# One hybrid layer on one core: the spill of the residual, the order of expert selection, and the layout of the sub keys changed

## The chip, the core and the metric

The program runs on 1 core of one Trainium2 chip. TensorE (PE) does the matrix products, VectorE (DVE) and ScalarE (ACT) the element-wise work, GpSimd (POOL) issues the gathers, and SyncE (SP) issues almost all other transfers, which 16 DMA engines carry out. The metric is the device time of one execution in microseconds (us), lower is better.

## What is computed

One layer on 512 tokens of 2048 features, float32. The first half (a retention branch and a dilated attention branch) yields `merged`. The change lies in the second half:

```python
x = x + merged @ w_out                       # residual
h2 = rms_norm(x, ffn_norm_g)
x = x + peer_ffn(h2, w_query, sub_keys, u, v)

def peer_ffn(h, w_query, sub_keys, u, v):    # 8 heads, 128 keys, 16384 experts
    q = (h @ w_query).reshape(B, S, 8, 256)
    s1 = einsum('bshd,hkd->bshk', q[..., :128], sub_keys[:, 0])
    s2 = einsum('bshd,hkd->bshk', q[..., 128:], sub_keys[:, 1])
    v1, i1 = top_k(s1, 16);  v2, i2 = top_k(s2, 16)
    best, pos = top_k(all sums v1 + v2, 16)
    experts = i1[pos // 16] * 128 + i2[pos % 16]
    gates = softmax(best)
    act = gelu(h . u[experts]) * gates       # 128 experts per token
    return sum of act * v[experts]
```

## The kernel before

The 512 tokens are four tiles of 128. The whole layer runs twice over its stages: part 0 for tile 0, part 1 for tiles 1 to 3. Tiles 0 and 1 then fetch the rows of their experts one by one with gathers (POOL, line 756; DVE multiplies each gathered row, lines 765 and 774, 2.3 us each). A gather step is let out by `tick` each time a part of a weight has been split (0.85 of a step) or a step of the gate tables is done (one step). Tiles 2 and 3 take another way: all 128 groups of 128 experts are multiplied out densely, which is the long last phase.

Matrix products use split numbers. `load_w` loads 256 rows of a weight (`wraw`, 512 KB, line 127, SP), ACT rounds it (`whi`, line 130) and DVE subtracts (`wlo`, line 131); three products per pair then go to PE (`gemm`, lines 146 to 148). One such weight part stands for 18 products of 128x512 with three tiles, and a chunk of 512 columns has eight parts. In the second half of the program there are four buffers for `wraw` and three for `whi` and `wlo`.

`merge` multiplies by `w_out` in four chunks (loop at 604). For each chunk and tile it loads the old residual (`xr`, line 609, three buffers), adds it to the product (line 610, DVE, written to `x1`), sends the sum to memory (`x1D`, line 611, SP), and squares it on ACT (line 612, into `xr`, with the sum of squares as a by-product). After the last chunk `x1` is scaled in place (line 623 on DVE for tiles 0 and 2, line 621 on ACT for tile 1), transposed (line 597), split (lines 567 and 568), and the first tile is multiplied by the norm's gains (`fgr`, lines 628 to 630, whose buffers are those of `xr`).

`routing` takes four chunks of queries. Each chunk c is a product with `w_query`, a copy (`qn`, 641), transposes (648, 650), scores against `skT` (653, 656), and then the selection on DVE: the top 16 of every half (lines 520 to 524), of their sums, a look-up of the expert numbers (695 to 703), and the softmax, whose exponential is on ACT (707). `routing_tables` (714 to 726) loads the sub keys in four pieces, transposes them on PE and copies them on ACT. Before the selection of chunk 3 the call `before_last` writes out the first NFIRST = 11 groups of dense experts (`expert_in`: `ur` from SP at 836, `uh` on ACT at 839, `ul` on DVE at 840, 48 products at 854 to 856). When the last selection is done, expert numbers and gates go through memory (`hk_T`, 888 to 900), and the stage of the gate tables `GD` follows, in four blocks of eight steps (912 to 928) with more dense experts between them. One further group closes the stage, so that 24 groups are done when the dense phase begins.

A scheduler orders each engine's instructions when the program is built; each engine then works through its own list strictly in that order, and waits where the next instruction waits. So the place of an instruction in a list decides what is held up behind it.

Of the kernel before, what the change touches and what calls it, by code (L numbers as in the profile page):

```python
# [10 lines left out]
F32 = mybir.dt.float32  # L11
BF16 = mybir.dt.bfloat16
F32R = mybir.dt.float32r
U32 = mybir.dt.uint32
I32 = mybir.dt.int32
AF = mybir.ActivationFunctionType
# [3 lines left out]
P = 128  # L20
# [6 lines left out]
H = 8  # L27
# [37 lines left out]
def hybrid_layer(ctx, tc, I, out, dbg=None):  # L65
    nc = tc.nc
# [33 lines left out]
    ident = const.tile([P, P], F32, name="ident")  # L100
# [3 lines left out]
    def bank(name, pool=None):  # L104
        return (pool or psB).tile([P, 512], F32, name=name, tag="bank")
# [49 lines left out]
    with tc.tile_pool(name="x0", bufs=1) as x0:  # L155
# [22 lines left out]
        for k in range(KT):  # L178
            ps = bank("xT")
# [25 lines left out]
    x1D = dram.tile([NT, P, D], F32, name="x1D")  # L205
# [334 lines left out]
    def merge(part, mg, pieces):  # L540


        t0, T = (0, 1) if part == 0 else (1, NT - 1)
# [34 lines left out]
        for c in range(4):  # L578
            cs = slice(c * 512, (c + 1) * 512)
            ps = gemm((I["w_ret_out"][0], c * 512, tiles(rT)))[0]  # L580
# [4 lines left out]
            ps = gemm((I["w_attn_out"][0], c * 512, tiles(aT)), nk=8)[0]  # L585
# [16 lines left out]
        ss4 = mg.tile([P, T, 4], F32, name="ss4")  # L602
        x1 = [mg.tile([P, D], F32, name=f"x1_{t}", tag=f"row{t}") for t in range(T)]
        for c in range(4):
            cs = slice(c * 512, (c + 1) * 512)
            ps = gemm((I["w_out"][0], c * 512, tiles(mT)))[0]
            for t in range(T):
                xr = mg.tile([P, 512], F32, name="xr", tag="xr", bufs=3)
                nc.sync.dma_start(xr, x4[t0 + t][:, cs])
                nc.vector.tensor_add(x1[t][:, cs], ps[t], xr)  # L610
                nc.sync.dma_start(x1D[t0 + t][:, cs], x1[t][:, cs])
                nc.scalar.activation(xr, x1[t][:, cs], AF.Square, accum_out=ss4[:, t, c:c + 1])
        fg = mg.tile([P, KT], F32, name="ffng")
        nc.sync.dma_start(fg, I["ffn_norm_g"][0].rearrange("(k p) -> p k", p=P))
        for t in range(T):
# [10 lines left out]
        for c in range(4):  # L626
            cs = slice(c * 512, (c + 1) * 512)
# [5 lines left out]
    def routing(T, rt, skT, tab, tiles2, before_last=None):  # L633

        N2 = 2 * T
        gates, e1, e2 = [rt.tile([P, T, 8, 16], F32, name=n, bufs=1) for n in ("gates", "e1", "e2")]
        for c in range(4):
            ps = paired((I["peer_w_query"][0], c * 512, tiles2))
            qn = rt.tile([P, T, 512], F32, name="qn", bufs=2)
            for t in range(T):  # L640
                nc.scalar.copy(qn[:, t], ps[t])
            v12 = rt.tile([P, T, 2, 2, 16], F32, name="v12")
            i12 = rt.tile([P, T, 2, 2, 16], U32, name="i12")
            scs = []
            for i in range(4):
                pt = bank("qT")
                for t in range(T):
                    nc.tensor.transpose(pt[:, t * P:(t + 1) * P], qn[:, t, i * P:(i + 1) * P], ident)
                qT = rt.tile([P, T * P], F32, name="qTs", bufs=2)
                nc.scalar.copy(qT, pt[:, :T * P])  # L650
                ss = bank("s12")
                for t in range(T):
                    nc.tensor.matmul(ss[:, t * P:(t + 1) * P], qT[:, t * P:(t + 1) * P], skT[:, 4 * c + i],
                                     start=True, stop=True)
                sc = rt.tile([P, T * P], F32, name="s12s", bufs=4)
                nc.scalar.copy(sc, ss[:, :T * P])
                scs.append(sc)
            if c == 3 and before_last:
                before_last()
            for i in range(4):  # L660
                for t in range(T):
                    scr = rt.tile([P, P], F32, name="scr")
# [14 lines left out]
            for a in range(N2):  # L677
# [32 lines left out]
            nc.vector.tensor_mul(gates.rearrange("p t (c u) k -> p t c u k", c=4)[:, :, c],  # L710
                                 ex.rearrange("p (t u) k -> p t u k", t=T),
                                 sm.rearrange("p (t u) -> p t u", t=T)[:, :, :, None].to_broadcast([P, T, 2, 16]))
        return e1, e2, gates

    def routing_tables(rt):
        tab = rt.tile([P, 3, 16], F32, name="tab", bufs=1)
        nc.sync.dma_start(tab.rearrange("p a b -> p (a b)"), bcast(I["c_rank"], 48))
        skT = rt.tile([P, 16, P], F32, name="skT", bufs=1)
        for q4 in range(4):
            sk = rt.tile([P, 4, P], F32, name="sk", bufs=1)  # L720
            nc.sync.dma_start(sk, I["peer_sub_keys"][0].rearrange("h s k d -> k (h s) d")[:, 4 * q4:4 * q4 + 4])
            ps = bank("skT")
            for i in range(4):
                nc.tensor.transpose(ps[:, i * P:(i + 1) * P], sk[:, i], ident)
            nc.scalar.copy(skT[:, 4 * q4:4 * q4 + 4].rearrange("p a b -> p (a b)"), ps)
        return skT, tab


# [63 lines left out]
    with tc.tile_pool(name="mgA", bufs=1, reuse_waits="tile") as mg, \  # L792
            tc.tile_pool(name="rtA", bufs=2, reuse_waits="tile") as rt, \
            tc.tile_pool(name="flA", bufs=2, reuse_waits="tile") as fl:
        skT, tab = routing_tables(rt)
# [24 lines left out]
    NV = 8  # L820
    NGRP = P // NV
    NPRE = 24
    NFIRST = 11
    NLAST = 1
    right = ctx.enter_context(ExitStack())
    pools = {}
# [38 lines left out]
    def begin_dense():  # L865
# [5 lines left out]
        load_u(0)  # L871
        for n in range(NFIRST):
            expert_in(n)

    with tc.tile_pool(name="mgO", bufs=1, reuse_waits="tile") as mgO:
# [5 lines left out]
        with tc.tile_pool(name="rtB", bufs=2, reuse_waits="tile") as rt:  # L881
            skT, tab = routing_tables(rt)
            e1, e2, gates = routing(3, rt, skT, tab, tiles2, begin_dense)
            unit(1, e1[:, 0], e2[:, 0], gates[:, 0], h2D)
            for i, src in enumerate((e1, e2, gates)):
                ps = bank("hkT")
# [8 lines left out]
    with tc.tile_pool(name="gb", bufs=1, reuse_waits="tile") as gb:  # L895
# [6 lines left out]
        for blk in range(NB):  # L902
# [3 lines left out]
            for o in range(TB // OB):  # L906
                t0 = blk * TB + o * OB
# [6 lines left out]
                for q in range(OB // 4):  # L914
                    ps = bank("gg")
# [101 lines left out]
def laid_out(inputs):  # L1017
    host = {n: np.ascontiguousarray(inputs[n]) for n in _INS}
    u = host["peer_u"].reshape(P, P, KT, P)
    host["u_feat"] = np.ascontiguousarray(u.transpose(0, 3, 2, 1)).reshape(P, P, KT * P)  # L1020
    host.update(shape_constants())
    return host

# [16 lines left out]
```

## Time and profile before

| | us |
|---|---|
| median of 3 runs (4589.60 to 4595.62) | 4591.96 |
| the profiled execution | 4602.08 |
| its span, first to last instruction | 4600.3 |
| stage: `w_out` of part 1 to the last sum | about 2600 to 2736 |
| stage: norm and transposes | 2736 to 2767 |
| stage: four query chunks and their scores | 2763 to 2968 |
| stage: dense experts up to the hand-over of the selection | 2968 to 3032 |
| stage: hand-over and gate tables | 3032 to 3271 |
| stage: dense phase | 3271 to 4600 |

Times in the trace count from the start of the span. In a timeline row the first number is the start, the second the duration; square brackets give how long the engine had stood idle before and what ended that. PEclk is the granted clock of TensorE as a share of 2.4 GHz, 0.5 being 1.2 GHz. A DMA share is the mean busy share of the 16 DMA engines.

### The profile page before, as it was taken

What the parts mean: (1) busy time and instruction counts of PE and PEld (TensorE: products, weight loads), DVE (VectorE), ACT (ScalarE), POOL (GpSimd) and SP (SyncE); (2) the same over time, 40 slices, a digit from 0 to 9 for tenths busy, and PEclk for the clock granted to TensorE, in tenths of its full rate; (3) what the DMA queues carried; (4) which work ended last, traced back from release to release, by engine and by line L of the source; (5) the groups of instructions that cost most, each with busy time, mean ns of one, the idle gap of its engine ahead of it and who ended that gap; (6) DMA issues with size and microseconds to landing.
All of it is one profiled execution on the core that took longest, in us unless ns stands there. A gap on an engine that the chain in (4) does not pass through costs nothing.

```text
span 4600.3 us, 57918 instructions
## 1 busy us (share of the span) xinstructions
PE 4211.8 (92%) x21638; PEld 3524.4 (77%) x21638; DVE 3439.3 (75%) x4495; ACT 1917.0 (42%) x2674; POOL 795.5 (17%) x516
## 2 busy tenths in 40 slices
PE   8999998988998999989979977886799999999999
PEld 6878776765776778767758866786689998899997
DVE  7454554546566878677678878888779998999997
ACT  6444555545442323443432333344434443344443
POOL 0000000000002112222122221012112332344332
PEclk9999999999999999999989998998899999999999
DMA  7666675758658889888899885267889999999997
GB/s 241 226 219 218 215 243 178 244 193 287 224 160 303 323 290 331 313 305 320 300 346 373 340 323 202 92 236 292 318 302 363 397 400 391 401 400 402 405 403 293
DMA packets 510171, 1358.78 MB, mean 295 GB/s; under 512 B 49216, under 2 KB 129088, under 8 KB 440768
## 3 DMA queue, kind: packets, MB, share of 16 engines
q1 hardware_dynamic: 432800, 816.00, 50.9%
q0 software_dynamic: 73728, 536.90, 29.7%
q8 instruction: 170, 2.79, 0.2%
q10 hardware_dynamic: 3360, 2.17, 0.2%
q14 instruction: 113, 0.93, 0.1%
HBM read 1290.05 MB, written 64.88 MB: 295 GB/s over the span
## 4 chain that ended last, share of the span: by engine, by line
PE 50%; DMA 18%; DVE 13%; issue 13%; ACT 3%; POOL 2%; SPq 0%; ACTq 0%; DVEq 0%; POOLq 0%
PE gB L147 9%; PE gB L148 9%; PE gB L146 9%; PE psy L981 3%; PE psy L982 3%; PE psy L980 3%; PE psa L856 3%; PE psa L854 3%; PE psa L855 3%; DMA gr<-in_peer_v,eid 3%; DMA ur<-in_u_feat 3%; DMA wraw<-in_w_in 2%; POOL gr L756 2%; DVE wlo L131 2%; DMA vr<-in_peer_v 2%
## 5 line engine op out<-in xcount | busy, mean ns | idle before, releaser
L131 DVE TENSOR_TENSOR wlo<-wraw,whi 128x1024 fp32r<-128x1024 f32 x752 | 917.2, 1223 | 650.6 <-ACT whi L130 636.0
L130 ACT CAST whi<-wraw 128x1024 fp32r<-128x1024 f32 x752 | 789.4, 1051 | 1227.7 <-PE gB L148 913.6
L756 POOL DMA_INDIRECT gr<-in_peer_u,eid x256 | 362.9, 1418 | 2752.8 <-DVE eid L743 1535.1
L774 DVE SCALAR_TENSOR_TENSOR accg<-gr,wg,accg 128x2048 f32<-128x2048 f32 x256 | 600.5, 2346 | 50.6 <-DMA gr<-in_peer_v,eid 38.5
L765 DVE SCALAR_TENSOR_TENSOR gr<-gr,hrow 128x2048 f32<-128x2048 f32 x256 | 583.8, 2284 | 45.7 <-DMA gr<-in_peer_u,eid 44.2
L854 PE MATMUL psa<-rh,uh 128*128 128x256 f32 x2048 | 582.1, 284 | 29.6 <-ACT uh L839 29.6
L756 POOL DMA_INDIRECT gr<-in_peer_v,eid x256 | 432.4, 1689 | 994.8 <-DVE accg L774 929.1
L856 PE MATMUL psa<-rh,ul 128*128 128x256 f32 x2048 | 581.8, 284 | 9.8 <-DVE ul L840 9.8
L855 PE MATMUL psa<-rl,uh 128*128 128x256 f32 x2048 | 580.0, 283 | 0.0
L839 ACT CAST uh<-ur 128x1024 fp32r<-128x1024 f32 x256 | 268.9, 1051 | 479.0 <-DMA ur<-in_u_feat 381.1
L981 PE MATMUL psy<-vl,wh 128*128 128x512 f32 x1024 | 405.1, 396 | 19.7 <-DVE vl L974 19.5
L854 PEld LDWEIGHTS psa<-rh,uh 128*128 128x128 f32 x2048 | 390.9, 191 | 34.7 <-ACT uh L839 30.5
L980 PE MATMUL psy<-vh,wh 128*128 128x512 f32 x1024 | 402.5, 393 | 6.0 <-ACT vh L973 5.9
L982 PE MATMUL psy<-vh,wl 128*128 128x512 f32 x1024 | 400.7, 391 | 0.0
L855 PEld LDWEIGHTS psa<-rl,uh 128*128 128x128 f32 x2048 | 397.6, 194 | 4.0
L856 PEld LDWEIGHTS psa<-rh,ul 128*128 128x128 f32 x2048 | 390.7, 191 | 12.2 <-DVE ul L840 12.0
L973 ACT CAST vh<-vr 128x1024 fp32r<-128x1024 f32 x256 | 267.9, 1050 | 300.6 <-DMA vr<-in_peer_v 164.5
L974 DVE TENSOR_TENSOR vl<-vr,vh 128x1024 fp32r<-128x1024 f32 x256 | 310.4, 1220 | 76.8 <-ACT vh L973 76.4
L147 PE MATMUL gB<-wlo,rh 128*128 128x512 f32 x768 | 316.3, 412 | 52.3 <-DVE wlo L131 52.0
L840 DVE TENSOR_TENSOR ul<-ur,uh 128x1024 fp32r<-128x1024 f32 x256 | 311.2, 1218 | 57.5 <-ACT uh L839 56.3
L146 PE MATMUL gB<-whi,rh 128*128 128x512 f32 x768 | 309.2, 406 | 31.5 <-ACT rh L570 22.7
L148 PE MATMUL gB<-whi,rl 128*128 128x512 f32 x768 | 311.0, 405 | 0.3 <-DVE rl L571 0.2
(467 smaller groups left out, 7957.5 us busy)
## 6 DMA issues: line engine op xcount, KB each, us to landing
wraw<-in_w_in SPq DMA_DIRECT2D x528, 512.0 KB, 5.0
ur<-in_u_feat SPq DMA_DIRECT2D x256, 512.0 KB, 9.6
vr<-in_peer_v SPq DMA_DIRECT2D x256, 512.0 KB, 9.9
wraw<-in_w_ret_out SPq DMA_DIRECT2D x64, 512.0 KB, 6.1
wraw<-in_w_out SPq DMA_DIRECT2D x64, 512.0 KB, 5.8
wraw<-in_peer_w_query SPq DMA_DIRECT2D x64, 512.0 KB, 4.9
wraw<-in_w_attn_out SPq DMA_DIRECT2D x32, 512.0 KB, 6.8
GD<-Gs SPq DMA_DIRECT2D x4, 4096.0 KB, 14.6
```

Source lines behind the costliest of these rows:

```text
L130: nc.scalar.copy(whi, raw)
L131: low = nc.vector.tensor_sub(wlo, raw, whi.bitcast(F32))
L146: nc.tensor.matmul(ps[t], ah(k), whi[:, j], start=first, stop=False)
L147: nc.tensor.matmul(ps[t], ah(k), wlo[:, j], start=False, stop=False)
L148: nc.tensor.matmul(ps[t], al(k), whi[:, j], start=False, stop=last)
L756: nc.gpsimd.indirect_dma_start(out=r, out_offset=None, in_=pu if s < P else pv_, in_offset=bass.IndirectOffsetOnAxis(ap=u.eid[:, s % P:s % ...
L765: nc.vector.scalar_tensor_tensor(r, r, 1.0, u.hrow, op0=ALU.mult, op1=ALU.mult, accum_out=u.ag[:, s:s + 1])
L774: nc.vector.scalar_tensor_tensor(u.acc, r, u.wg[:, s - P:s - P + 1], u.acc, op0=ALU.mult, op1=ALU.add)
L854: nc.tensor.matmul(psa[:, j], uh[:, cs], chi[k], start=k == 0, stop=False)
L855: nc.tensor.matmul(psa[:, j], uh[:, cs], clo[k], start=False, stop=False)
L856: nc.tensor.matmul(psa[:, j], ul[:, cs], chi[k], start=False, stop=k == KT - 1)
L981: nc.tensor.matmul(ps[:, t], wh[:, j, ts_], vl[:, j], start=False, stop=False)
```

## The change

Four edits.

1. The spill. The sum of line 610 is written into the loaded tile `xr`, and `x1D` is stored from there. ACT squares `xr` into `x1` and then copies `xr` to `x1`. `xr` is the buffer that the next loads of `xr` and `fgr` take.
2. The order of selection. `routing` is cut into `queries(c)` and `select(c)`, written in the order queries 0, queries 1, select 0, queries 2, select 1, queries 3, first dense experts, select 2, select 3. The scores `s12s` have eight buffers in place of four.
3. NFIRST is 16 in place of 11.
4. The host lays out the sub keys as `key_feat` (feature by key), and one transfer of 1 MB fills `skT`.

```diff
-                nc.vector.tensor_add(x1[t][:, cs], ps[t], xr)
-                nc.sync.dma_start(x1D[t0 + t][:, cs], x1[t][:, cs])
-                nc.scalar.activation(xr, x1[t][:, cs], AF.Square, accum_out=ss4[:, t, c:c + 1])
+                nc.vector.tensor_add(xr, ps[t], xr)
+                nc.sync.dma_start(x1D[t0 + t][:, cs], xr)
+                nc.scalar.activation(x1[t][:, cs], xr, AF.Square, accum_out=ss4[:, t, c:c + 1])
+                nc.scalar.copy(x1[t][:, cs], xr)
...
-        for c in range(4):
+        def queries(c):
+
             ps = paired((I["peer_w_query"][0], c * 512, tiles2))
...
-            v12 = rt.tile([P, T, 2, 2, 16], F32, name="v12")
-            i12 = rt.tile([P, T, 2, 2, 16], U32, name="i12")
             scs = []
...
-                sc = rt.tile([P, T * P], F32, name="s12s", bufs=4)
+                sc = rt.tile([P, T * P], F32, name="s12s", bufs=8)
                 nc.scalar.copy(sc, ss[:, :T * P])
                 scs.append(sc)
-            if c == 3 and before_last:
-                before_last()
+            return scs
+
+        def select(c, scs):
+            v12 = rt.tile([P, T, 2, 2, 16], F32, name="v12")
+            i12 = rt.tile([P, T, 2, 2, 16], U32, name="i12")
...
+        found = {}
+        for c in range(4):
+            found[c] = queries(c)
+            if c == 3 and before_last:
+                before_last()
+            if c > 0:
+                select(c - 1, found.pop(c - 1))
+        select(3, found.pop(3))
         return e1, e2, gates
...
-        for q4 in range(4):
-            sk = rt.tile([P, 4, P], F32, name="sk", bufs=1)
-            nc.sync.dma_start(sk, I["peer_sub_keys"][0].rearrange("h s k d -> k (h s) d")[:, 4 * q4:4 * q4 + 4])
-            ps = bank("skT")
-            for i in range(4):
-                nc.tensor.transpose(ps[:, i * P:(i + 1) * P], sk[:, i], ident)
-            nc.scalar.copy(skT[:, 4 * q4:4 * q4 + 4].rearrange("p a b -> p (a b)"), ps)
+        nc.sync.dma_start(skT, I["key_feat"].rearrange("d (a k) -> d a k", a=16))
         return skT, tab
...
-    NFIRST = 11
+    NFIRST = 16
...
+    keys = host.pop("peer_sub_keys").reshape(2 * H, P, P)
+    host["key_feat"] = np.ascontiguousarray(keys.transpose(2, 0, 1)).reshape(P, 2 * H * P)
```

SP's list at the change from the second to the third chunk of `w_out` in part 1, before (`wraw` are weight parts, `x1D` the stores, `xr` the loads of the old residual):

```order
L611 DMA x1D<-x_0_19291 128x512
L611 DMA x1D<-x_1_19292 128x512
L609 DMA xr<-in_x 128x512 x2
L611 DMA x1D<-x_2_19293 128x512
L127 DMA wraw<-in_w_out 128x2x512
L609 DMA xr<-in_x 128x512
L127 DMA wraw<-in_w_out 128x2x512 x7
```

and after the change:

```order
L611 DMA x1D<-xr 128x512 x2
L609 DMA xr<-in_x 128x512
L611 DMA x1D<-xr 128x512
L127 DMA wraw<-in_w_out 128x2x512
L609 DMA xr<-in_x 128x512 x2
L127 DMA wraw<-in_w_out 128x2x512 x7
```

The rows are nearly the same, but a load of `xr` now takes a buffer from which a store was just issued, and it stands ahead of the third store and of eight weight parts.

DVE's list at the start of the selection of chunk 0 in part 1, before (`wlo` are weight parts, `accg` the use of a gathered row, the MAX and MATCH rows the selection):

```order
L131 TENSOR_TENSOR wlo<-wraw,whi 128x1024
L774 SCALAR_TENSOR_TENSOR accg<-gr,wg,accg 128x2048
L131 TENSOR_TENSOR wlo<-wraw,whi 128x1024
L520 MAX v_20699<-s12s 128x8 x2
L521 MAX_INDEX i_20700<-v_20699,s12s 128x8
L522 MATCH_REPLACE scr<-v_20699,s12s 128x128
L521 MAX_INDEX i_20700<-v_20699,s12s 128x8
```

and, some 30 selection rows in, after the change:

```order
L524 MAX_INDEX i_20970<-v_20969,scr 128x8
L131 TENSOR_TENSOR wlo<-wraw,whi 128x1024
L780 SCALAR_TENSOR_TENSOR accg<-gr,wg,accg 128x2048
L522 MATCH_REPLACE scr<-v_20969,s12s 128x128
L520 MAX v_20969<-s12s 128x8
L131 TENSOR_TENSOR wlo<-wraw,whi 128x1024
L780 SCALAR_TENSOR_TENSOR accg<-gr,wg,accg 128x2048
L523 MAX v_20969<-scr 128x8
```

Before, the next weight part stood behind 88 selection rows; now the five parts that chunk 1 still lacks stand among the first 44 rows, and the first four of chunk 2 in the selection's last steps.

ACT's list around the scores of chunk 3, before (`qn`, `qTs`, `s12s` as above, `uh` the dense experts' rounding):

```order
L641 COPY qn<-gB 128x512 x3
L650 COPY qTs<-qT 128x384
L656 COPY s12s<-s_21911 128x384
L650 COPY qTs<-qT 128x384
L839 CAST uh<-ur 128x1024
L656 COPY s12s<-s_21923 128x384
L650 COPY qTs<-qT 128x384
```

and after the change:

```order
L643 COPY qn<-gB 128x512 x3
L650 COPY qTs<-qT 128x384
L656 COPY s12s<-s_21717 128x384
L650 COPY qTs<-qT 128x384
L710 ACTIVATE ex<-ex 128x96
L845 CAST uh<-ur 128x1024
L656 COPY s12s<-s_21729 128x384
```

The exponential of the selection of chunk 2 now stands ahead of the first `uh` and of three of the four score copies of chunk 3.

## Rows read from the trace of the kernel before

**Rows 1.** The page: busy time by engine, TensorE's clock, DMA share by slices.

```profile
PE 4211.8 (92%) x21638; PEld 3524.4 (77%) x21638; DVE 3439.3 (75%) x4495; ACT 1917.0 (42%) x2674; POOL 795.5 (17%) x516
...
PEclk9999999999999999999989998998899999999999
DMA  7666675758658889888899885267889999999997
```

**Rows 2.** Busy time of each engine by stretches; the first line names the columns.

```profile
core 0: us, PE busy (x) PEld busy (x) DVE busy (x) ACT busy (x) POOL busy (x), PEclk, DMA share, GB/s
2640.00:2720.00 80.00, 74.95 (x322) 59.81 (x321) 54.61 (x38) 21.55 (x29) 19.79 (x14) 1.00 0.93 354
...
2801.30:2960.30 159.00, 124.63 (x543) 98.07 (x540) 144.20 (x534) 40.31 (x59) 10.79 (x7) 0.89 0.34 119
...
2968.30:3032.30 64.00, 61.49 (x523) 60.92 (x522) 57.68 (x173) 29.23 (x32) 1.68 (x1) 0.97 0.59 202
3032.30:3046.00 13.70, 13.70 (x119) 13.70 (x118) 4.90 (x4) 6.57 (x9) 0.00 (x0) 1.00 0.66 213
3046.00:3091.40 45.40, 30.02 (x217) 28.03 (x217) 41.93 (x64) 23.09 (x53) 13.28 (x7) 0.81 0.61 227
...
3271.00:4600.00 1329.00, 1295.40 (x7992) 1161.06 (x7992) 1194.14 (x980) 532.89 (x577) 420.38 (x224) 0.99 0.98 376
```

**Rows 3.** Timeline of all engines at the norm of part 1.

```profile
2732.01 0.94 SPq L611 DMA_DIRECT2D x1D<-x  x2
...
2738.94 0.28 DVE L619 RECIPROCAL ssx<-ssx 128x1 f32<-128x1 f32 x3
...
2744.03 1.29 DVE L623 TENSOR_SCALAR x<-x,ssx 128x2048 f32<-128x2048 f32 x1 [4.81 <-DMA x1D<-x]
...
2745.81 2.00 ACT L621 ACTIVATE x<-x,ssx 128x2048 f32<-128x2048 f32 x1 [7.63 <-DMA x1D<-x]
...
2749.07 1.29 DVE L623 TENSOR_SCALAR x<-x,ssx 128x2048 f32<-128x2048 f32 x1 [3.75 <-DMA wraw<-in_peer_w_query]
```

**Rows 4.** DMA issues, 2600 to 2770: count, KB each, median us to landing.

```profile
x1D<-x SPq DMA_DIRECT2D x12, 256.0 KB, 11.9
...
fgr<-in_ffn_norm_g SPq DMA_DIRECT2D x4, 256.0 KB, 14.0
...
wraw<-in_w_out SPq DMA_DIRECT2D x25, 512.0 KB, 8.8
```

**Rows 5.** The sub keys' transposes on PE: part 1 grouped, part 0's first.

```profile
L724 PE MATMUL skT<-ident,sk 128*128 128x128 f32 x16 | 3.0, 317 | 6.4 <-DMA sk<-in_peer_sub_keys 6.4
...
993.11 1.12 PE L724 MATMUL skT<-ident,sk 128*128 128x128 f32 x4 [8.54 <-DMA sk<-in_peer_sub_keys]
```

**Rows 6.** PE's timeline: first transpose after chunk 0, a stall, after chunk 3.

```profile
2801.16 0.38 PE L648 MATMUL qT<-ident,qn 128*128 128x128 f32 x2
...
2825.95 0.79 PE L147 MATMUL gB<-wlo,rh 128*128 128x512 f32 x1 [6.74 <-DVE wlo L131]
...
2960.15 0.38 PE L648 MATMUL qT<-ident,qn 128*128 128x128 f32 x2
```

**Rows 7.** Query products alone by stretches: PE, PEld, DVE, ACT, clock, DMA, GB/s.

```profile
2801.30:2810.10 8.80, 5.46 (x19) 3.15 (x19) 0.00 (x0) 0.59 (x1) 1.00 0.70 254
2801.30:2960.30 159.00, 114.55 (x433) 86.12 (x432) 0.00 (x0) 5.28 (x9) 0.89 0.34 119
```

**Rows 8.** DVE's timeline: the first selection's start, and the row behind its end.

```profile
2804.93 0.49 DVE L520 MAX8 v<-s12s 128x8 f32<-128x128 f32 x2 [0.78 <-ACT s12s L656]
...
2845.82 1.22 DVE L131 TENSOR_TENSOR wlo<-wraw,whi 128x1024 fp32r<-128x1024 f32 x1
```

**Rows 9.** The page's groups: the use of a gathered row on DVE.

```profile
L774 DVE SCALAR_TENSOR_TENSOR accg<-gr,wg,accg 128x2048 f32<-128x2048 f32 x256 | 600.5, 2346 | 50.6 <-DMA gr<-in_peer_v,eid 38.5
```

**Rows 10.** SP's timeline: the stores of the first and last block of gate tables.

```profile
3091.37 0.32 SPq L928 DMA_DIRECT2D GD<-Gs  x1
...
3253.14 0.33 SPq L928 DMA_DIRECT2D GD<-Gs  x1
```

## The prediction

> **What bounds the kernel now.** I read the busy totals first. PE is busy 92% of the span, at a clock near full [rows 1], so time can be won only where PE stands idle or slow. Next the busy times by stretch. The last 1329 us keep PE busy 97% at clock 0.99, with the DMA engines at 0.98 [rows 2]. None of the edits reaches there, so that stage stays as it is. What is left lies between the `w_out` chunks and 3271. There the DMA slices fall from 8 and 9 to 5 and 2 [rows 1], and the stretches give the reason: the query chunks 1 to 3 last 159.0 us with PE busy 124.6 and DVE busy 144.2, at a DMA share of 0.34 [rows 2]. DVE is the limit there, not loads. The dense experts behind them run with PE busy 61.5 of 64.0 [rows 2]. The block of gate tables after that has PE busy 30.0 of 45.4 at clock 0.81 [rows 2]: room that moved experts leave or fill.
>
> **The change part by part**, against the profiled execution (4602.1).
>
> (a) The spill. The reciprocal stands at 2738.94, ready at 2739.2. DVE scales tile 0 only at 2744.03, after 4.81 us of waiting for the store of `x1`, ACT tile 1 at 2745.81, DVE tile 2 at 2749.07 [rows 3]. That last one ends at 2750.4; its named releaser is a weight load, but the store of tile 2 is as late, and I take that for the cause. Without the waits the two scalings on DVE would end at 2739.2 + 2 × 1.29 = 2741.8, a gain of 8.5. But DVE's new list has the multiplication with the first `fgr` right behind the second pair of splits, and `fgr` now lands in a buffer that a store has to leave. The store of tile 0 issued at 2732.01 and its landing released DVE at 2744.0 [rows 3]. Issued there, and with an estimate of 4 us for its landing in an emptying queue (the median in this stretch is 14.0 [rows 4]), `fgr` is there at 2748. About 3.5 of the 8.5 remain. Bounds: −8.5 (`fgr` early), +4 (the two last `fgr` wait for the third store, which itself issues some 8 us later). The twelve extra copies on ACT are hidden: ACT is busy 21.6 of 80 us there [rows 2]. **−3.5.**
>
> (b) The sub keys. In part 1 PE's transposes took 3.0 and idled 6.4 for the four pieces [rows 5]. Both go, and the one load issues ahead of the weight parts behind chunk 0, with some 30 us until the first scores need it. In part 0 PE idled 8.54 before its first transposes [rows 5]; other inputs were late there as well, so I take −1 (−3 to +2, the big load being ahead of others in the queue). **−10.4**, bounds −13 to −4.
>
> (c) Chunks 1 to 3. From the end of chunk 0 (2801.2) to that of chunk 3 (2960.2) [rows 6] are 159.0. Undisturbed, a chunk costs 8.8 for its first 19 products, which lie between the transposes and scores of the chunk before [rows 7], and 125 more at 74.95 / 322 = 0.233 [rows 2] = 29.1, so 37.9, for three 113.7. 45 us are lost, in waits such as 6.74 for a `wlo` that stands behind a selection [rows 6]. A selection costs DVE 2845.82 − 2804.93 = 40.9 [rows 8], less two `wlo` and two uses of gathered rows at 1.22 and 2.35 [rows 8, 9] = 33.8. I went down DVE's new list with these durations, one weight part of PE being 18 × 0.233 = 4.2, and a `wlo` not before its buffer's user three parts earlier is done. Chunk 1 gets its five missing parts early and runs through. In chunk 2 PE waits 3.7, 6.2 and 1.2 for parts that stand in the tail of the selection, in chunk 3 0.7 and 4.7: 16.5 in all. 113.7 + 16.5 = 130, so 29 less. The same walk over the old list puts the end of chunk 3 at 2961.9, where the trace has 2960.2. **−29**, bounds 0 (the waits come back elsewhere) and −45 (none left).
>
> (d) The hand-over from chunk 3 to the experts took 8.1 (2960.2 to 2968.3). ACT now must do the exponential of selection 2 before it copies three of the four scores and rounds the first `uh`. By the walk, DVE has that input 5 us after ACT could start. Behind ACT wait the score products and the first experts on PE. **+4**, bounds 0 to +8.
>
> (e) Five more dense groups ahead of the hand-over. 64.0 us held 523 products, 48 per group: 5.87 each [rows 2]. **+29.4**, on the path, since by the walk DVE is through selection 3 at about 3020 and PE through 16 groups at about 3037, before (a) and (b).
>
> (f) Fewer groups later. Before, three groups covered the way of the tables through memory (3032.3 to some 3050, PE full in its first 13.7 us [rows 2]) and nine stood in the three blocks behind. Now two cover it, and five are left in the blocks. The cover costs nothing: the way itself sets the time. The stores of first and last block lie 161.8 apart [rows 10], 53.9 per block with three groups; the block without took 45.4 [rows 2]. 8.5 / 3 = 2.84 per group, four groups: **−11.4**. Bounds: −8 by the smallest difference of one block, −19 if the 45.4 hold 4 us of filling.
>
> (g) `w_out`. SP now waits at a load of `xr` until a store has landed, with the third store and weight parts queued behind it, and PE waits for those. At the second and third chunk change two such waits follow each other: 2 × 11.9 = 23.8, then 8.8 for the weight part [rows 4] and 2.3 for its split: 34.9. PE has seven parts at 4.2 = 29.4 ahead of it. Late by 5.5, twice, if landings stay 11.9; but they are long because the queue is full (DMA share 0.93 [rows 2]), and a waiting SP empties it. **+3**, bounds 0 and +30 (below). The Trainium skill, page "DMA: Bandwidth & Descriptors", section "Latency and other measured facts", puts the fixed cost of a transfer at about 2 us, growing with the load on memory. By that price two waits would be an estimated 4 us and this term nothing; the 11.9 measured here speaks against it.
>
> Sum: −3.5 − 10.4 − 29 + 4 + 29.4 − 11.4 + 3 = −17.9. 4602.1 − 17.9 = 4584. The profiled execution lay 10.1 above the median of 4592.0; the median should move by as much: **4574**.
>
> **The rivals.**
>
> *More.* If all 45 us of (c) go and a group in (f) costs 4.8: −16 and −8 more, 4574 − 24 = 4550. For it: DMA is nearly idle in that stretch, and the parts are loaded. Against it: DVE's list still puts three parts of chunk 2 behind a tail.
>
> *No difference.* The waits move from `wlo` to `ul`: DVE's work, 144 of 159 us busy [rows 2], does not shrink, and 27 `ul` now stand before the end of selection 3 in place of 19. If experts crawl at DVE's pace, half of (c) is given back, 14.5, and the end is 4588 to 4590. For it: DVE was busy 57.7 of 64.0 in the old experts' stretch [rows 2]. Against it: PE was full there all the same.
>
> *Slower.* SP's waits in (g). At each of the two chunk changes SP stands for 23.8 us. What it queued before, two weight parts at 8.8 at most, keeps the engines busy for half of that; the remaining 15 are lost for a stream that uses 0.93 of the engines, and PE gets its parts later by that much. 2 × 15 = 30 in place of 3: −17.9 + 27 = +9, 4601. It decides from 13.5 us per change. For it: the share of 0.93. Against: gathers use the engines too and would go ahead meanwhile, and seven parts of cover. The Trainium skill, page "Perfetto Trace Analysis", section "Optimization Strategy", takes a gap that repeats over a stretch as a sign of too few buffers; here that would be a repeated gap at each chunk change, with three `xr` buffers held by stores. The trace before shows no such gap (PE busy 74.95 of 80 [rows 2]).
>
> *The spill's edit does not do what it says*: scaling begins early, but `fgr` holds DVE until 2750. Then (a) is 0, and the time 4577.
>
> **How the numbers follow.** About 0.2%, 9 us, is what a measurement of this kernel can tell from no change. My sum 0.52 (own range 4560 to 4586), more 0.13, no difference 0.17, slower 0.11, the spill without gain 0.07. From my sum 0.44 lie below 4582.8 and 0.08 above; more adds 0.13 and the spill's case 0.06 to faster, no difference 0.03. Faster 0.66, within 0.22 (0.08, 0.01 and 0.13), slower 0.12 (0.11 and 0.01). The range reaches down to the rival's 4550 and a little below, 4546, and up to 4598, which leaves out most of the slower case and the rest of the bounds of (c).
>
> **What would show it.** (a) the scaling starting near 2739 on its own stage's clock and an idle DVE ahead of the first `fgr` product. (b) no PE idle time between query products of chunk 0. (c) about 130 us from the last product of chunk 0 to that of chunk 3, the waits in chunk 2 after the selection's tail. (d) ACT idle before an exponential ahead of `uh`. (e) 768 products before the hand-over at 0.12 us each. (f) blocks of about 50 us. (g) SP waiting for a store at `xr`, PE idle for under 6 us per chunk change. I would be wrong above all if PE ran no faster through chunks 2 and 3, if experts were paced by `ul`, or if `w_out` stalled.

## The result: 1.0% faster, more than twice the forecast step

The median went from 4593.8 us (4 runs, 4589.6 to 4602.4) to 4550.5 (4 runs, 4541.0 to 4557.4). The ratio is 0.9902 with a 95% interval of 0.9875 to 0.9929, so 45 us less, 33 to 57. The forecast was 18 less and 4574; its range held the time at its lower edge, the likeliest case's own range (4560 to 4586) did not. The direction was right; the forecast step was less than half of the measured one.

The profiled execution after took 4544.0, with a span of 4542.2; the one before took 4602.1. So 58 us lie between the two traces, and 43 to 45 between the kernels. Single stages vary from trace to trace even where the code is the same: the `w_out` chunks of part 1 took 125.5 to 132.2 in ten traces with the same code there, and the stage from the reciprocal to the last norm transpose 17 to 25 in nine. The table therefore has, beside the two traces, the means over the traces of this study that lack and that have the edit in question (their number in brackets). In the last three rows that is the old order with 11 groups against 16 groups in either order, in the last with the store on SP alone; the run with buffers of its own for `fgr` is not counted in (a). Stages run from one event to the next, in part 1; the first one begins with the last transpose of `merged`.

| stage, and the prediction's letter | forecast | before | after | mean without | mean with | change of means |
|---|---|---|---|---|---|---|
| `w_out` products (g) | +3 | 130.5 | 125.5 | 125.6 (4) | 128.8 (10) | +3.2 |
| reciprocal to last norm transpose (a) | -3.5 | 24.1 | 19.5 | 24.4 (4) | 21.3 (9) | -3.1 |
| to the end of chunk 0 (b) | -9.4 | 38.1 | 26.9 | 38.9 (3) | 26.9 (11) | -12.0 |
| chunks 1 to 3 (c) | -29 | 159.0 | 128.4 | 158.3 (4) | 128.0 (10) | -30.3 |
| to the first dense group (d) | +4 | 4.6 | 7.8 | 4.6 (4) | 7.8 (10) | +3.1 |
| dense groups to the hand-over (e) | +29.4 | 67.5 | 94.5 | 67.9 (3) | 94.9 (3) | +27.0 |
| hand-over to first table product (f) | 0 | 17.6 | 15.3 | 17.8 (3) | 14.5 (3) | -3.3 |
| tables to first product of the dense phase (f) | -11.4 | 231.1 | 209.4 | 235.0 (3) | 208.1 (2) | -26.9 |

The changes of the means add up to -42, near the 43 to 45 of the timed runs. Seven of the eight rows came out within 3.5 us of the forecast. The last is off by 15.

The page after, with the lines that answer to [rows 1]:

```profile
PE 4205.8 (93%) x21606; PEld 3524.3 (78%) x21606; DVE 3436.5 (76%) x4495; ACT 1928.2 (42%) x2682; POOL 802.2 (18%) x516
...
PEclk9999998999999999999989999988899999999999
DMA  7666675758657888888889896358889999999997
```

PE has almost the same work in 58 us less. Busy times by stretch, as in [rows 2]: one inside the `w_out` chunks, chunks 1 to 3, the dense groups ahead of the hand-over, the dense phase:

```profile
core 0: us, PE busy (x) PEld busy (x) DVE busy (x) ACT busy (x) POOL busy (x), PEclk, DMA share, GB/s
2627.00:2707.00 80.00, 79.95 (x349) 64.96 (x348) 59.55 (x40) 26.01 (x36) 21.45 (x15) 1.00 1.00 381
2772.75:2901.20 128.45, 117.97 (x541) 95.23 (x540) 124.91 (x461) 40.22 (x58) 8.69 (x7) 0.96 0.46 164
2909.00:3003.50 94.50, 93.39 (x784) 92.09 (x785) 86.72 (x216) 44.02 (x49) 1.81 (x1) 0.98 0.55 191
...
3228.20:4542.20 1314.00, 1288.47 (x7944) 1156.26 (x7944) 1188.45 (x974) 536.20 (x572) 411.67 (x224) 0.99 0.98 377
```

In the chunks PE's clock rose from 0.89 to 0.96, and PE's busy time fell by 6.7 us for the same products: the waits ahead of PE's products fell from 34.4 us to 10.5 (sums of PE's waits in the chunks), and the products after them took less time. The dense phase is 5 us shorter in this trace, but over the traces with 24 groups ahead of it that phase took 1307 to 1326; no edit reaches it.

The norm after, all engines, the answer to [rows 3]:

```profile
2726.41 0.27 DVE L620 RECIPROCAL ssx<-ssx 128x1 f32<-128x1 f32 x3
2726.60 2.48 DVE L624 TENSOR_SCALAR x<-x,ssx 128x2048 f32<-128x2048 f32 x2
...
2728.03 2.87 PE L597 MATMUL mT<-ident,x 128*128 128x128 f32 x12 [11.76 <-DVE x L624]
2728.24 0.33 SPq L630 DMA_DIRECT2D fgr<-in_ffn_norm_g  x1
...
2733.40 0.69 DVE L631 TENSOR_TENSOR x<-x,fgr 128x512 f32<-128x512 f32 x1 [2.73 <-DMA fgr<-in_ffn_norm_g]
...
2734.63 0.82 PE L597 MATMUL mT<-ident,x 128*128 128x128 f32 x3 [2.80 <-DVE rl L568]
```

The scaling starts with the reciprocal. The first `fgr` issues 8.8 us after the stores at 2719.47, as one of them lands, and DVE waits 2.73 for it, with the splits behind it and PE waiting for those. That is step (a) as the prediction put it; the four `fgr` landed 3.4 to 6.2 us after issue, where it had 4 without a row for it.

PE's waits for weight parts in chunks 1 to 3, and ACT's and PE's rows behind chunk 3:

```profile
2814.53 0.50 PE L147 MATMUL gB<-wlo,rh 128*128 128x512 f32 x1 [2.57 <-DVE wlo L131]
...
2831.76 0.79 PE L147 MATMUL gB<-wlo,rh 128*128 128x512 f32 x1 [4.58 <-DVE wlo L131]
...
2863.10 0.51 PE L147 MATMUL gB<-wlo,rh 128*128 128x512 f32 x1 [3.32 <-DVE wlo L131]
...
2907.70 0.28 ACT L710 ACTIVATE ex<-ex 128x96 f32<-128x96 f32 x1 [2.93 <-DVE ex L709]
...
2908.97 0.58 PE L860 MATMUL psa<-rh,uh 128*128 128x256 f32 x1 [2.89 <-ACT uh L845]
```

Chunk 1 runs through, chunk 2 has two waits and chunk 3 one, 10.5 us where the walk had 16.5. The rest of the three chunks is PE's busy time, 118.0, where the walk had 113.7. ACT does wait for the exponential's input ahead of `uh`, 2.93 where the walk had 5.

SP's waits from 2620 to 2740 (engine, line, what for: us in all, times, longest):

```profile
SPq L609 <- DMA x1D<-xr: 29.5, 8, 7.8
...
SPq L630 <- DMA x1D<-xr: 13.7, 3, 7.8
```

SP does stand for the stores. The DMA engines are busy all the same (share 1.00, 381 GB/s above, against 0.93 and 354 in [rows 2]), and PE waits 0.8 us in all. In the other traces with this edit PE's waits there are 1.2 to 5.2, so the edit may cost some; the trace before has 5.1, the other three without the edit none.

The stores of the four blocks of gate tables, as in [rows 10]:

```profile
3061.19 0.32 SPq L934 DMA_DIRECT2D GD<-Gs  x1
...
3106.03 0.33 SPq L934 DMA_DIRECT2D GD<-Gs  x1
...
3152.50 0.33 SPq L934 DMA_DIRECT2D GD<-Gs  x1
...
3199.34 0.33 SPq L934 DMA_DIRECT2D GD<-Gs  x1
```

44.8, 46.5 and 46.8, where before 161.8 lay between the first and the last [rows 10], 53.9 per block. Here the miss lies.

### The profile page after: what moved, and what is told of

Its sections match the earlier page's. It is cut to its first block, busy times and chain, and to the rows that moved or that the text cites. A ratio compares the mean times of both kernels' runs of the same rounds, so it can differ in the third digit from the quotient of the medians.

```text
span 4542.2 us, 57820 instructions
## 1 busy us (share of the span) xinstructions
PE 4205.8 (93%) x21606; PEld 3524.3 (78%) x21606; DVE 3436.5 (76%) x4495; ACT 1928.2 (42%) x2682; POOL 802.2 (18%) x516
## 4 chain that ended last, share of the span: by engine, by line
PE 46%; issue 23%; DMA 13%; DVE 9%; POOL 6%; ACT 3%; SPq 0%; POOLq 0%; ACTq 0%; DVEq 0%
PE gB L147 10%; PE gB L148 10%; PE gB L146 10%; POOL gr L762 6%; DMA wraw<-in_w_in 3%; PE psa L862 2%; PE psa L860 2%; PE psa L861 2%; PE psy L987 2%; PE psy L988 2%; PE psy L986 2%; DVE wlo L131 2%; DMA gr<-in_peer_u,eid 2%; ACT whi L130 2%; DVE gr L771 1%
```

## The experiments

The kernel before took 4596 to 4600 by the median beside these runs; ratios are against its runs on the same chip.

### One edit at a time

The first kernel has the spill's edit alone:

```diff
-                nc.vector.tensor_add(x1[t][:, cs], ps[t], xr)
-                nc.sync.dma_start(x1D[t0 + t][:, cs], x1[t][:, cs])
+                nc.vector.tensor_add(xr, ps[t], xr)
+                nc.sync.dma_start(x1D[t0 + t][:, cs], xr)
```

> The kernel before with the spill's edit alone. Theory (the stages add, each edit keeps its own share): the scaling starts right behind the reciprocal, PE's idle time ahead of the norm's transposes falls from 16.4 us to about 12 plus some 3 for fgr, the w_out chunks are no slower: 4.5 us less, some 4589. Rival (SP's waits at xr cost in w_out and eat it): the way from the first w_out product to the reciprocal, 140.6 before, grows by 6 or more and the time is the same or longer. Third reading: if the 5 us by which w_out was shorter in the changed kernel belong to this edit, 9 to 10 us less.

Measured: 0.9989 (0.9979 to 0.9998), 5 us less. PE's idle time ahead of the norm's transposes is what it is in the kernel after, and the stage (a) took 22.2. The `w_out` stretch took 126.1, as in the kernel after and not longer than in the trace before; so the rival with SP's waits is out as a large loss. The third reading falls too: kernels without this edit have 123.8 to 130.5 there, so the 5 us between the first two traces were chance.

The second has the new order and the one load of the keys, with 11 groups and the old spill:

```diff
-                sc = rt.tile([P, T * P], F32, name="s12s", bufs=4)
+                sc = rt.tile([P, T * P], F32, name="s12s", bufs=8)
...
+            if c > 0:
+                select(c - 1, found.pop(c - 1))
+        select(3, found.pop(3))
...
+        nc.sync.dma_start(skT, I["key_feat"].rearrange("d (a k) -> d a k", a=16))
```

> The kernel before with the new order of selection and the one load of the sub keys; NFIRST stays 11, the spill stays as it was (the new order does not fit beside the buffers of the four key pieces, so the two go together). Theory: the end of chunk 3 comes 30 us earlier by the order and 11 by the keys, but the last selection on DVE then ends only shortly after PE is through 11 groups, so PE waits a little at the hand-over, and the hand-over comes some 36 to 41 us earlier; the blocks of gate tables stay as before (220.8 from the hand-over to the last store): about 4555. Rival (groups moved ahead are what pays): PE waits for the last selection by 15 us or more, and the time is 4570 or above.

Measured: 0.9940 (0.9925 to 0.9955), 28 us less, 4565: between the two. The chunks took 128.4, the full 30 less. But at the hand-over PE meets the selection (the profiled execution took 4554.6, the fastest of the six), as these rows of its transposes show (PE's timeline, the products of the dense groups that lie between them left out):

```profile
2971.74 0.44 PE L893 MATMUL hkT<-ident,e 128*128 128x128 f32 x2 [1.75 <-DVE e L702]
...
2979.23 0.44 PE L893 MATMUL hkT<-ident,e 128*128 128x128 f32 x2 [1.40 <-DVE e L705]
...
2979.51 0.38 PE L893 MATMUL hkT<-ident,gates 128*128 128x128 f32 x2
```

The last transposes come 7.8 us after the first, with DVE as the one waited for, where the trace before has all six within 0.8, and the way to the first table product is 22.6 where it was 17.6. The 16 us that remain beyond the keys are about half of what the chunks gained.

The third has the keys alone:

```diff
-            nc.sync.dma_start(sk, I["peer_sub_keys"][0].rearrange("h s k d -> k (h s) d")[:, 4 * q4:4 * q4 + 4])
...
+        nc.sync.dma_start(skT, I["key_feat"].rearrange("d (a k) -> d a k", a=16))
```

> The kernel before with the one load of the sub keys alone. Theory: no transposes of keys on PE, the stretch from the last norm transpose to the end of chunk 0 falls from 38.1 to 27, hand-over 11 us earlier, in all 11 to 12 us less: about 4582. Rival (DVE bounds the chunks, so the gain is given back there): chunk 0 ends earlier by 11 but the end of chunk 3 by less than 5, time within 4 us of before.

Measured: 0.9975 (0.9964 to 0.9987), 11.5 us less. The stretch to the end of chunk 0 is 26.9 in place of 38.1, and chunks 1 to 3 keep their 158.2. The theory held, and the gain is not given back there.

The fourth has the 16 groups alone:

```diff
-    NFIRST = 11
+    NFIRST = 16
```

> The kernel before with NFIRST 16 alone. Theory A (a group in the gate-table blocks costs little until the block's third, which costs a lot): hand-over 29 us later, from hand-over to the last store 196 in place of 220.8, net +4 us, about 4598. Theory B (the prediction's price, 2.84 us for each group in the blocks): +29.4 - 11.4 = +18, about 4612. Theory C (a group costs its 5.9 us of PE wherever it stands): within 3 us of before, with every block shorter by 5.9 for each group taken out.

Measured: 0.9993 (0.9982 to 1.0004), 3 us less, no clear difference. B, the prediction's price, is out: it asked for 18 more. The hand-over comes 27 us later by its stage (94.7 in place of 67.5), and the three blocks took 44.0, 47.3 and 46.9 in place of 55.9, 54.3 and 51.6. They are shorter by 11.9, 7.0 and 4.7. By the dense products that PE started in them (70, 96 and 96 in place of 142, 144 and 142, with 48 to a group) that is for one and a half, one and one groups less: the list does not keep the groups in the blocks where the program writes them. C asks for 8.8, 5.9 and 5.6, 20 in all, where 23.6 were measured; A asks for 25 from the hand-over to the last store, where 28 were measured. Neither is out by this run.

### What a group in a block costs

The changed kernel with 11 groups:

```diff
-    NFIRST = 16
+    NFIRST = 11
```

> The changed kernel with NFIRST back at 11. Theory (the third group of a block is dear, and with the new order the last selection on DVE ends after PE has run 11 groups, so the groups moved ahead fill a wait): from the first dense group to the hand-over 70 in place of 94.5, hand-over to the first table product 22 in place of 15, blocks 54 to 56 each in place of 45 to 47: 13 us longer than the changed kernel, about 4564. Rival (the prediction's prices, 5.87 ahead and 2.84 in a block): 18 us shorter, about 4533.

Measured: 0.9911 (0.9891 to 0.9931), 4560. The rival is out: it is not shorter. By stages it is as the theory had it: 70.0 to the hand-over, 22.4 to the first table product, blocks of 56.3, 54.2 and 55.1. From the first dense group to the first product of the dense phase the trace has 330 us against 319 with 16. The timed runs, though, differ by 4 us only, with an interval too wide to tell 0 from 13.

With 15 groups, so that all blocks have two:

```diff
-    NFIRST = 16
+    NFIRST = 15
```

> The changed kernel with NFIRST 15, so that the blocks have two groups each. Theory (the first two groups of a block cost some 2.3 us each): one group less ahead of the hand-over, -5, one more in the second block, +2.3: 3 us less than the changed kernel, about 4548. By the prediction's prices 3 less as well; if a group costs 5.9 everywhere, no difference; if the second group of a block is as dear as the third, 3 more.

Measured: 0.9911 (0.9892 to 0.9930), 4556, no measurable difference to 16. The blocks took 48.5, 47.2 and 47.5.

With 13, so that two and three groups stand in one program:

```diff
-    NFIRST = 16
+    NFIRST = 13
```

> The changed kernel with NFIRST 13: blocks of two, three, two and three groups in one program, the first block's two being the cover of the way through memory. Theory T (the price of a group is a step: the first two of a block are cheap, the third dear): second and fourth block 54 to 56, third 46 to 48. Rival L (the price is even, and the long blocks of the kernel before were long for another reason, such as the place of the gathers): all three blocks within 2 us of each other, at about 50.

Measured, in one execution: 56.4 and 55.1 with three groups, 50.0 with two between them. The block with two is the shorter one, as T asked, but 2 to 4 longer than T had it, and the difference of 5.1 to 6.4 would fit C's 5.9 as well. L's even 50 is out. DVE's waits in the second block (three groups) and in the third (two), from their stores:

```profile
DVE ul L846 <- ACT uh L845: 7.8, 3, 2.8
```

```profile
DVE ul L846 <- ACT uh L845: 3.6, 1, 3.6
```

Over all traces with 24 groups and the store on SP, seventeen blocks with three groups took 51.6 to 56.4, 55.0 in the mean; eleven with two 46.5 to 50.0, mean 47.7. So the third group costs 7.3, more than C's 5.9. The two shortest blocks, 44.0 and 44.8 (the first one each with 16 groups), are 3.3 shorter than those with two; they hold 70 dense products, three loads of `ur` and two `ul`, that is one to one and a half groups. So the second group costs between 3.3 and 6.6, and that it is much cheaper than the third, as T has it, is not shown by the times.

DVE's waits do show a step. In the seventeen blocks with three groups it waits 4.8 to 8.9 us for `uh`, 7.1 in the mean; in the eleven with two 0 to 3.6, 1.2 in the mean; in the two shortest not at all.

What the stretch held that the prediction took for a block without groups, and the three blocks behind it (dense products alone: PE, PEld and ACT busy with counts, clock, DMA share, GB/s; before):

```profile
3046.00:3091.40 45.40, 11.88 (x89) 10.78 (x89) 0.59 (x1) 0.81 0.61 227
3091.40:3147.30 55.90, 20.36 (x144) 19.12 (x143) 1.18 (x2) 0.78 0.73 282
3147.30:3201.60 54.30, 20.52 (x146) 19.17 (x145) 0.60 (x1) 0.84 0.75 286
3201.60:3253.10 51.50, 21.00 (x142) 19.95 (x142) 1.18 (x2) 0.90 0.78 305
```

It was not without: 89 products are 1.85 groups, where the others hold three.

### Why the third is dear

DVE's waits over the three blocks, in the trace before (3091.4 to 3253.1):

```profile
DVE ul L840 <- ACT uh L839: 19.8, 8, 2.9
```

and in the trace after (3061.2 to 3199.3):

```profile
DVE oh L918 <- PE gg L930: 5.8, 5, 1.8
...
DVE gr L771 <- DMA gr<-in_peer_u,eid: 1.5, 1, 1.5
```

Before, DVE stood 19.8 us for `uh`; after, not at all. Add seven `ul` less (17 and 10), which start 1.14 apart, 8.0, and take off 4.3 for the difference of the other waits (5.8 and 1.5 here, 3.0 for gathered rows before): 23.5, where the blocks lost 161.8 - 138.1 = 23.7. ACT in turn waits for the loads `ur` (17.5 us over the three blocks before), which issue right behind the 4 MB store. First attempt at that: the store from another queue, with 11 groups and with 16.

```diff
-            nc.sync.dma_start(GD[blk], Gs)
+            nc.scalar.dma_start(GD[blk], Gs)
```

> As the run with all edits and NFIRST 11, but the 4 MB store of a block's gate tables is issued by ACT, so that it is in another queue than the loads of ur. Theory Q (the third group is dear since the loads of ur queue behind the store on SP, and DVE's list then waits for uh): the landing of ur behind a store falls from 12 us to 5, DVE's waits for uh in a block from 8 us to under 3, the blocks with three groups take 47 to 50 in place of 54 to 56, about 20 us less in the stage. Rival D (the DMA engines have 4 MB to move in any case): ur lands no sooner, the blocks stay at 54 to 56.

> The changed kernel (NFIRST 16) with the store of the gate tables issued by ACT. Theory Q: blocks with one or two groups lose 2 to 3 us of waits for ur each, the stage 6 to 9 us shorter, about 4543. Rival D: no difference, 4550.

Measured: 0.9926 (0.9908 to 0.9943) and 0.9913 (0.9891 to 0.9934), neither better. With 11 groups the stage from the first table product to the first product of the dense phase grew from 237.9 to 249.7, with 16 from 209.4 to 218.8. Waits of DVE, then of ACT, over the blocks with 11 groups:

```profile
DVE ul L846 <- ACT uh L845: 32.6, 8, 7.6
```

```profile
ACT uh L845 <- DMA ur<-in_u_feat: 61.8, 8, 17.6
```

Theory Q fell. The first load behind the second store, with 11 groups, from issue to landing (the last figure, us): with the store on SP, then on ACT:

```profile
ur<-in_u_feat SPq DMA_DIRECT2D x1, 512.0 KB, 18.7
```

```profile
ur<-in_u_feat SPq DMA_DIRECT2D x1, 512.0 KB, 16.2
```

Behind the first three stores such a load took 17.4 to 19.6 us on the store's own queue and 16.2 to 18.6 beside it, about as long as the store itself (14.6 to 18.4), and not the 5 that Q asked for. The Trainium skill, page "DMA: Bandwidth & Descriptors", section "Issuing engines are not separate DMA queues", says that transfers issued by different engines run on the same DMA engines and interleave, so that a second issuer saves only the time of issuing. This run agrees, with 16.2 to 18.6 against 17.4 to 19.6.

That the stage grew goes with the order of ACT's list, by the rows; no run has the one without the other. ACT's rows behind the second store, issued by SP and issued by ACT:

```profile
3102.57 1.28 ACT L926 ACTIVATE oh<-oh,hkT 128x128 f32<-128x128 f32 x4 [3.67 <-DVE oh L919]
3107.54 1.28 ACT L926 ACTIVATE oh<-oh,hkT 128x128 f32<-128x128 f32 x4 [3.69 <-DVE oh L919]
...
3118.08 1.04 ACT L845 CAST uh<-ur 128x1024 fp32r<-128x1024 f32 x1 [1.64 <-DMA ur<-in_u_feat]
```

```profile
3101.28 0.33 ACTq L934 DMA_DIRECT2D GD<-Gs  x1
3118.87 1.04 ACT L845 CAST uh<-ur 128x1024 fp32r<-128x1024 f32 x1 [17.62 <-DMA ur<-in_u_feat]
```

With the store in ACT's list, `uh` stands right behind it, and the table steps that ACT did while the load was on its way now stand behind `uh`. So these two runs test the landing, and not what an earlier landing would be worth.

Second attempt: more loads ahead. To make room for more buffers, both kernels have 8 groups less ahead of the dense phase (16 in all, three ahead of the hand-over and three written in each block; the first of the three blocks held two and a half, by its products), one with three buffers of `ur` and one with five:

```diff
-    NPRE = 24
-    NFIRST = 16
+    NPRE = 16
+    NFIRST = 3
...
-            ur = pools["d1"].tile([P, 1024], F32, name="ur", bufs=3)
+            ur = pools["d1"].tile([P, 1024], F32, name="ur", bufs=5)
```

> The changed kernel with 16 groups in place of 24 ahead of the dense phase, three of them ahead of the hand-over and three in each block (8 groups move into the dense phase, which makes room for more buffers). Three buffers of ur, as ever. Both theories: PE waits for the selection at the hand-over, and the blocks take 52 to 56 as with three groups each in the kernel before. It is the reference for the next run.

> The same with five buffers of ur. Theory B (the third group is dear since only three half-groups can be on their way while the 4 MB store of the block before holds the DMA engines): ACT's waits for ur and DVE's for uh in a block fall under 3 us, and the blocks take 46 to 49. Rival D (the engines' work in the block sets the landing, whenever the load is issued, or ACT and PE are too slow for three groups beside eight steps): the blocks stay at 52 to 56.

Measured, in one execution each: blocks of 51.3, 54.0 and 55.2 with three buffers, 47.2, 50.2 and 50.2 with five. Over the three blocks, with three buffers (DVE, then ACT):

```profile
DVE ul L846 <- ACT uh L845: 17.1, 8, 2.7
```

```profile
ACT uh L845 <- DMA ur<-in_u_feat: 19.0, 9, 2.7
```

and with five:

```profile
DVE ul L846 <- ACT uh L845: 7.7, 4, 4.3
...
DVE oh L918 <- PE gg L930: 2.2, 2, 1.7
```

```profile
ACT uh L845 <- PE psa L861: 14.9, 8, 4.7
ACT uh L845 <- DMA ur<-in_u_feat: 7.7, 5, 2.3
```

Two more buffers take 13.0 us off three blocks, 9.4 of them from DVE's waits. That is theory B, in part: the late loads cost 4.3 us per block, of the 7.3 that the third group costs. The waits did not all fall under the 3 us that B asked for. About 2.3 are the group's own two `ul` on DVE. What is left of `uh`'s waits then is for PE, which has to free the buffers of `uh`. The two executions took 4577 and 4549 us in all, one each, which is no comparison of the kernels.

### The gains' loads out of the way

15 groups, and in part 1 four buffers for `fgr` alone:

```diff
-            fgr = mg.tile([P, 512], F32, name="fgr", tag="xr", bufs=3)
+            fgr = mg.tile([P, 512], F32, name="fgr", tag="xr" if part == 0 else "fgr", bufs=3 if part == 0 else 4)
```

> The changed kernel with NFIRST 15 and, in part 1, four buffers of its own for fgr, so that its loads no longer wait for a store to leave xr. Theory: DVE's wait for the first fgr in the norm (2.8 us of PE idle time) goes, reciprocal to last norm transpose 17 in place of 17 to 22, all else as with NFIRST 15: 3 us less than that, about 4550 by the median. Rival (fgr's landing is late for the queue's sake, not for the buffer's): the wait stays.

Measured: 0.9924 (0.9910 to 0.9938), 4558, no better than 15 groups alone. In the trace the wait is gone (PE's and DVE's rows at the norm):

```profile
2733.35 2.87 PE L597 MATMUL mT<-ident,x 128*128 128x128 f32 x12 [11.73 <-DVE x L624]
...
2735.89 0.68 DVE L631 TENSOR_TENSOR x<-x,fgr 128x512 f32<-128x512 f32 x1
...
2737.29 0.84 PE L597 MATMUL mT<-ident,x 128*128 128x128 f32 x3
```

and the stage (a) took 16.2, 5 less than the mean of the others, though one of those has 17. So the buffer is what held `fgr`, but 3 to 5 us are too little to be seen in the time. No version here is measurably better than the changed kernel.

## Why the prediction was right, and where it was short

*What bounds the kernel.* Right. The dense phase stayed, and all that moved by the means lies between `w_out` and the first product of the dense phase.

*(a)* Right in mechanism and size: -3.5 forecast, -3.1 by the means of stages that vary by more than that, with the wait for `fgr` that the new list promised. The run with buffers of its own confirms the cause.

*(b)* Right, a little small: -12.0 in part 1, where the idle time and the transposes gave 9.4. Alone it was worth 11.5 in time. The -1 for part 0 does not show: its first norm transpose starts at 1162.6 to 1163.8 in three traces with the four pieces and at 1162.8 to 1167.8 with the one load.

*(c)* Right: -29 forecast, -30.3. The walk down DVE's new list had the waits in chunks 2 and 3, if not each at its place. That the size came out so near is in part luck: the waits were 6 us fewer than in the walk, and the products took 4.3 more. Pricing the list with durations from the trace, after the same walk had reproduced the old end, was the best step of the prediction.

*(d), (e)* +33.4 forecast, +30.1. The trace before has its first dense product at 2964.8 and not at 2968.3, so (d) grew from 4.6 and not from 8.1. A group more ahead of the hand-over cost 5.4 and not 5.87.

*(g)* Small, as forecast: +3.2 by the means, with a spread between traces larger than that, so that its sign is not shown. SP waited as described.

*(f)* The step that failed: its price of 2.84 for a group taken out of a block. It took the stretch of 45.4 us ahead of the first store for a block without groups and divided the 8.5 that the others take more by three. That stretch held 1.85 groups of dense products (its 217 in [rows 2] are 128 for the tables and 89 dense ones), so the 8.5 stood for about 1.1 groups, 7.6 each. That this is near the 7.3 measured between blocks of three and two is in part chance: the stretch also held 12 uses of gathered rows on DVE where the others have 16. What makes the third group dear stood in the trace before as well, in DVE's 19.8 us of waits for `uh` in those blocks; only the stage's lengths were read, not its waits. With the hand-over the term measured -30 in place of -11.4. Its lower bound was off in itself: with 4 us of filling taken off the 45.4, it would be 12.5 / 3 × 4 = 16.7 and not 19.

"The way itself sets the time" failed too. Before, PE had no wait ahead of the first table product: it was busy for all of the 17.6 us, so three groups were longer than the way through memory. After, with two, PE waits for the way:

```profile
3018.79 1.62 PE L930 MATMUL gg<-oh,oh 128*128 128x128 f32 x6 [3.71 <-DVE oh L918]
```

So the group taken out of the cover shortened this stretch, by 3.3 in the means.

The terms add to -18 as forecast and -42 as measured. (f) makes 19 of the 24 that are missing; (e) 2.4, (b) 1.6, (c) 1.3, (d) 0.9, less 0.6 for (a) and (g).

*The rivals.* "More" named the right time, 4550, for a wrong main reason: two thirds of it were the rest of (c), which stayed. Its smaller part, a dearer group in (f), was the true one and still too small. The range reached down to the measured time for that rival's sake, so that it held is in part luck. "No difference" fell: 16 groups ran in 94.5 us, PE busy 93.4, so `ul` did not pace them. "Slower" fell: SP stood as described, and the DMA share in the chunks did not fall (1.00 against 0.93). The spill did what it says.

*Together and apart.* Alone the edits are worth 5, 11.5 and 3, and order with keys 28. The order's 30 us in the chunks come out at 16. In the two traces with the new order, 11 groups and the store on SP, the means of the stages behind the chunks are longer by 14 than in the old order: 4.6 from the hand-over to the first table product, where the last selection on DVE is waited for, 3.1 ahead of the first dense group, 2.2 in the dense groups and 4.1 from the tables on. That the five moved groups fill the wait at the hand-over, and shorten the blocks, is what the traces show (319 against 330 us from the first group to the dense phase); the timed runs are too coarse to confirm it.

## What to carry to other kernels

Price what is taken out of a stage at the margin: count what each stretch that you compare really holds, and look at what waits in the longest and the shortest, before you divide a difference by a number from the program text. In a list that each engine works through in order, walk the new list with durations from the trace, and let the same walk reproduce the old time first. A gain of a few microseconds is seen in the trace and not in the time when single executions differ by ten; compare several traces before giving a difference a cause.

## What the runs showed that was not expected

The first load of 512 KB issued behind a 4 MB store took 14.9 to 20.5 us to land in ten traces, whichever engine issued the store, while the store took 13.4 to 19.1. Moving the store into ACT's list lengthened the longest wait for a load there from 2.5 to 17.6 us with 11 groups, by the place of the next instructions and not by the landing. A waiting SP cost little in `w_out`: with 29.5 us of waits for stores there, the DMA share in 80 us of those chunks was 1.00. And PE's clock in the chunks, 0.89 of 2.4 GHz where PE waited 34.4 us, was 0.96 where it waited 10.5, so that the same products took 6.7 us less of PE's time.
